# When the left half's last sums, a pair's weight parts, the last x roundings and the first x loads run: four places in the order of a two-layer transformer trunk

## The chip, the cores and the metric

The kernel runs on one core of one Trainium2 chip. The metric is device time in microseconds (us) of one execution. Five engines work side by side, each through its own instructions in order: PE (matrix products), DVE and ACT (elementwise work), POOL (small elementwise work and some transfers) and SP (which only asks for transfers). An engine that waits holds back everything that stands behind the waiting instruction in its own order. Transfers asked for by SP, ACT or POOL run on the core's DMA engines.

## The reference

Two layers over 256 rows of 2048 numbers, everything in float32. Cut to what matters:

```
for l in range(2):
    h = rmsnorm(x, attn_norm_g[l])
    q, k, v, gate_b, gate_c, conv_in = split(h @ w_in[l])       # 6 x 1024 columns
    attn = diff_attention(norm(q), norm(k), v, lam, rel_bias)    # 8 heads
    conv = gate_b * causal_conv3(gate_c * conv_in)
    x = x + concat([attn, conv]) @ w_out[l]
    hm = rmsnorm(x, mlp_norm_g[l]) @ w_up[l]                     # 2048 -> 8192
    x = x + square(relu(hm)) @ w_down[l]                         # 8192 -> 2048
```

## The kernel before

Precision is kept by splitting each float32 operand into a rounded part ("hi") and the remainder ("lo"), so that each product is three matrix products: hi by hi, hi by lo, lo by hi (`TERMS`). ACT writes the hi part (`whi`, `uhi`, `t24h`), then DVE subtracts it from the raw tile for the lo part (`wlo`, `ulo`, `t24l`): lines 311 and 312 for plain weight tiles, 799 and 800 for `w_up`, 823 and 824 for the parts of a seven-product pair, 276 and 278 for the activations `nT` (a transposed, gained and rounded chunk of x).

**Weight tiles.** `Weights.take` hands PE the next hi and lo tile and prepares three further ones (`AHEAD`); the tiles `whi` and `wlo` have three buffers each. The order in which tiles are prepared can differ from that in which they are used: `weights.order`.

**The MLP.** The hidden width is cut into 32 pairs of 128 rows (`NP`). In a first pass the up projection of pair i and the down products of pair i-2 for the left 1024 output columns run together. In a second pass the down products for the right 1024 columns follow from hidden tiles that were stored to memory and are read again (`g`, `f`, `h`). In the second pass 13 pairs (`SEVEN`: 4, 6, 8, 10 ...) are computed as seven half-size products instead of eight: their weights come in three parts, `plain` (b1, b2), `sums` (t1, t3) and `more` (t2, t4), made from the raw tile with DVE lines 837, 840, 841 and rounded on 823 and 824. The other 19 pairs (`PLAIN`) use two plain weight tiles each, 12 matrix products a tile. So before the first seven-product pair PE uses the plain tiles of pairs 0 to 3; they are called tile 1 to tile 8 below. The table `slots` says after which plain tile a part of a seven-product pair is prepared; for the first of these pairs the list in front of it is written out by hand (`[mine[0], mine[1], mine[5], mine[3]]`, for plain, sums, the hidden tile, more).

**The left half's end.** Between the passes, the left columns of x get two additions: `onto` (line 1061, scaled products read from PSUM, the matrix products' accumulators) and then four additions of e tiles (line 1092: 128x512 each). In the last layer the left half is then stored to `out` on SP's queue (line 1096).

**The last chunk of x in the MLP's norm.** `Norm.chunk` transposes a chunk of x on PE and rounds it in four slices k = 0 to 3 with `split_gained` (ACT line 276, DVE line 278). For the last chunk (n = 3), PE's up projection comes to these slices right away, in the order of k.

**The mixer.** q, k and v are projected by halves. `qk_norm` transposes the normed q after a count of ticks (`yield 11`); PE calls `work.tick()` after each six matrix products, and the attention of the first half runs in between on the same ticks. Transposes and scores share three PSUM tiles called `bank`, in rotation: a new one waits until the tile three before it has been read. `Norm.factors` sends the row scales through PE (`rbc`, line 535) after `yield 5`.

**The start.** The first chunk of x is loaded in two halves, then `w_in`'s first tiles slice by slice (line 347, called K tiles here), then the rest (`first_loads`).

PE's order is the program's own; the orders of the other engines come from a scheduler that places instructions by its own model of time, except where the program pins one instruction behind another (`behind`, `late`).

Of the kernel before, what the change touches and what calls it, by code (L numbers as in the profile page):

```python
# [17 lines left out]
D = 2048  # L18
S = 256
# [9 lines left out]
CH = 512  # L29
WC = 256  # L30
KG = 4
# [77 lines left out]
def trunk(ctx: ExitStack, tc: tile.TileContext, x, w_in, w_out, conv_w, q_norm_g, k_norm_g,  # L109
          lambda_q1, lambda_k1, lambda_q2, lambda_k2, subln_g, attn_norm_g, mlp_norm_g,  # L110
          w_up, w_down, rel_bias, selector, out):
    nc = tc.nc
# [40 lines left out]
    ngv = const.tile([NG, P], F32, tag="ngv", name="ngv")  # L153
    load_x(0, 0, CH // 2)
    nc.scalar.dma_start(ngv, attn_norm_g.rearrange("l (k p) -> (l k) p", p=P))
    load_x(0, CH // 2, CH, nc.scalar)

    ones = const.tile([P, P], F32, tag="ones", name="ones")
    nc.vector.memset(ones, 1.0)
# [137 lines left out]
    class Weights:  # L297
# [36 lines left out]
        def plain(self, w, row, c, nk):  # L334

            cols = 2 * CH // nk

            def make():
                raw = self.early.pop(0) if self.early else load()
                return self.halves(raw)  # L340

            def load():
                raw = self.pool.tile([P, nk, cols], F32, tag="raw", name="raw", bufs=RAW)
                src = w[row:row + nk * P, c:c + cols].rearrange("(k p) c -> p k c", p=P)
                if row < KG * P and self.turns and not self.used:
                    for k in range(nk):
                        nc.sync.dma_start(raw[:, k], src[:, k])
                else:
                    self.loads.append(nc.sync.dma_start(raw, src))
                return raw  # L350

            make.load = load
            self.jobs.append(make)
# [89 lines left out]
    class Norm:  # L443
# [9 lines left out]
        def chunk(self, n, wait, banks=None):  # L453
            yield wait
            a = self.tiles[n].open()
            for j in range(2):
                tp = banks[j] if banks else bank(f"tpn{n}_{j}")
                for i in range(2):
                    k = 2 * j + i
                    for t in range(NT):  # L460
                        nc.tensor.transpose(
                            tp[:, i * S + t * P:i * S + (t + 1) * P],
                            xs[n][:, t, k * P:(k + 1) * P], ident)
                with tc.high_priority() if self.which and n == D // CH - 1 else ExitStack():
                    for i in range(2):
                        k = 2 * j + i
                        self.mark = split_gained(
                            a, k, tp[:, i * S:(i + 1) * S], norm_gain(self.which, self.l, n * KG + k))
                self.tiles[n].ready = 2 * j + 2
            self.squares(n)  # L470

# [35 lines left out]
        def factors(self):  # L507
            while self.squared < D // CH or not all(t.ready == KG for t in self.tiles):
                yield 1
            tot = small.tile([P, NT], F32, tag="tot", name="tot")  # L510
            nc.vector.tensor_reduce(tot, self.ss, axis=AX.X, op=ALU.add)
            r = rstd_of(tot, D, "row", NT)
            self.r = small.tile([P, NT], F32, tag="rowf", name="rowf", bufs=2)
            nc.vector.tensor_copy(self.r, r)
            diag = small.tile([P, NT * P + 32], F32, tag="diag", name="diag", bufs=1)
            diag = diag[:, :NT * P].rearrange("p (t c) -> p t c", t=NT)
            if self.which:

                self.scale = small.tile([P, 1], F32, tag="rowf2", name="rowf2")
                nc.vector.tensor_mul(self.scale, r[:, 1:2], r[:, 1:2])  # L520
                ratio = small.tile([P, 1], F32, tag="ratio", name="ratio")
                nc.vector.reciprocal(ratio, r[:, 1:2])
                nc.vector.tensor_mul(ratio, ratio, r[:, 0:1])
                nc.vector.tensor_scalar_mul(diag[:, 0], ident, ratio)
                yield 9
                tp = bank("rbc")
                nc.tensor.matmul(tp[:, :P], ones, diag[:, 0], start=True, stop=True)
                self.ratio = small.tile([P, P], F32, tag="rowb", name="ratiob", bufs=1)
                nc.vector.tensor_copy(self.ratio, tp[:, :P])
                return  # L530
            for t in range(NT):
                nc.vector.tensor_scalar_mul(diag[:, t], ident, self.r[:, t:t + 1])
            yield 5
            tp = bank("rbc")
            nc.tensor.matmul(tp[:, :S], ones, diag.rearrange("p t c -> p (t c)"),
                             start=True, stop=True)
            self.across = small.tile([P, 2, S], F32, tag="rowb", name="rowb", bufs=1)
            nc.vector.tensor_copy(self.across[:, 0], tp[:, :S])
            nc.gpsimd.tensor_tensor(self.across[:, 1], self.across[:, 0], self.across[:, 0],
                                    op=ALU.mult)  # L540
# [2 lines left out]

            return self.across[:, power - 1].unsqueeze(1).to_broadcast([P, 2, S])

    def qk_norm(acc, r, dst, gain, name):

        out_ = []
        for t in range(NT):
            rt = r[:, t:t + 1]  # L550
            sq = wide(f"{name}sq{t}")
            nc.scalar.activation(sq, acc[:, t], AF.Square, scale=rt)
            ms = small.tile([P, NH], F32, tag="ms", name=f"{name}ms{t}")
            nc.vector.tensor_reduce(ms, sq.rearrange("p (g d) -> p g d", d=DK),
                                    axis=AX.X, op=ALU.add)
            f = rstd_of(ms, DK, f"{name}{t}", NH)
            f2 = small.tile([P, NH], F32, tag="f2", name=f"{name}f{t}")
            nc.vector.tensor_scalar_mul(f2, f, rt)
            qn = wide(f"{name}n{t}")
            nc.vector.tensor_tensor(  # L560
                qn.rearrange("p (g d) -> p g d", d=DK),
                acc[:, t].rearrange("p (g d) -> p g d", d=DK),
                f2.unsqueeze(2).to_broadcast([P, NH, DK]), op=ALU.mult)
            out_.append(qn)
        yield 11
        for t in range(NT):
            tp = bank(f"{name}tp{t}")
            for i in range(4):
                nc.tensor.transpose(tp[:, i * P:(i + 1) * P], out_[t][:, i * P:(i + 1) * P], ident)
            tp3 = tp.rearrange("p (h c) -> p h c", c=P)  # L570
            hi, lo = (dst[:, i, :, t * P:(t + 1) * P] for i in range(2))
            nc.scalar.activation(hi, tp3, AF.Copy, scale=gain)
            nc.vector.scalar_tensor_tensor(lo, tp3, gain, hi.bitcast(F32),
                                           op0=ALU.mult, op1=ALU.subtract)
            yield 1
# [113 lines left out]
    def mixer(l, norm, loads):  # L689

        with ExitStack() as scope:
# [24 lines left out]
            for half in range(2):  # L716
# [2 lines left out]
                r = norm.r  # L719
                qT = (spare if half else cats).tile([P, 2, 4, S], F32R, tag=("c1", "s2")[half],  # L720
                                                    name=f"qT{l}{half}")
                work.start(qk_norm(acc, r, qT, q_gain[:, l:l + 1], f"q{l}{half}"))
                acc = linear(f"k{l}{half}", hT, weights)
                kT = (spare if half else cats).tile([P, 2, 4, S], F32R, tag=("c2", "s3")[half],
                                                    name=f"kT{l}{half}")
# [36 lines left out]
    def mlp(l, mnorm, ahead, last):  # L762
# [3 lines left out]
        with ExitStack() as scope:  # L766
# [117 lines left out]
            for i in range(NP - LAG, NP):  # L884
# [7 lines left out]
                   if i not in WHOLE}  # L892
            both = {i: dram.tile([P, 2, 7, P], F32R, name=f"both{l}_{i}") for i in WHOLE}
            plain = [dram.tile([P, 2, 2, 4, P], F32R, name=f"plain{l}_{b}")
                     for b in range((len(PLAIN) + 1) // 2)]
            again = {}

            def load_again(i):
                if i in WHOLE:
                    f = again[i] = fpool.tile([P, 2, 8, P], F32R, tag="f", name="f")  # L900
                    nc.gpsimd.dma_start(f[:, :, 1:], both[i])
                    return
                again[i] = tile_of("h", [P, 8, P], F32, (fpool, "h"), (second, "h"))
                nc.sync.dma_start(again[i][:, 1:].rearrange("p a c -> p (a c)"), hid[i])
# [22 lines left out]
            slots = {}  # L927
            for i in SEVEN:
                before = [j for j in mine if j < where[i]][-4:] if i != SEVEN[0] else [
                    mine[0], mine[1], mine[5], mine[3]]  # L930
                js = [where[i] + k for k in (1, 2, 0, 3)]
                if len(before) == 4 and SEVEN.index(i) and where[SEVEN[SEVEN.index(i) - 1]] > before[0]:
                    before = [before[2], before[2], before[3], before[3]]
                for j, b in zip(js, before):
                    slots.setdefault(b, []).append(j)
# [117 lines left out]
            def block(b):  # L1053
                blocks[b] = apool.tile([P, 2, 2, 4, P], F32R, tag="a", name="g")
                for s in range(min(2, len(PLAIN) - 2 * b)):
                    nc.gpsimd.dma_start(blocks[b][:, s], plain[b][:, s])

            block(0)

# [28 lines left out]
                    work.tick()  # L1088
            for dst, (_, _, p) in zip(left, OWN):
                onto(dst, prods[p], dst)  # L1090
            for dst, v in sums:
                nc.vector.tensor_add(dst, dst, v)

            def store(n):
                for t in range(NT):
                    nc.sync.dma_start(
                        out[0, t * P:(t + 1) * P, n * CH:(n + 1) * CH], xs[n][:, t])

            if last:
                store(0)  # L1100
                store(1)

            w2 = mm.tile([P, 2, CH], F32, tag="mm2", name=f"rt{l}2")
            prods[2], prods[3] = w2[:, 0], w2[:, 1]
# [2 lines left out]
            for i in range(NP):  # L1107
                if i in SEVEN:
# [19 lines left out]
                    if end:  # L1128
                        for dst, v in shared(*right):
                            nc.vector.tensor_add(dst, dst, v)  # L1130
                        if not last:
                            spare = (prods[7], prods[5])
                            work.start(norm.chunk(0, 2, spare), 2)
                            work.start(norm.chunk(1, 2, spare), 6)
                    continue
                b, slot = divmod(PLAIN.index(i), 2)
                if slot == 0 and b == 0:
                    with tc.issue_after(stored[-1].ins):
# [76 lines left out]
```

## Time and profile before

| | |
|---|---|
| median of 3 runs | 2144.89 us (2144.7 to 2146.6) |
| the profiled execution, its own time | 2145.36 us |
| its span, first to last instruction | 2143.5 us |
| mean granted PE clock | 0.999 |
| DVE busy | 1690.7 us (79%) |
| ACT busy | 1292.7 us (60%) |
| DMA, mean over the span | 228 GB/s |

A row of the timeline reads: start in us, duration in us, engine, line, operation, out<-in, count, and in square brackets the idle time before it and what ended it. A row of the chain of waits reads: start, duration, engine, tile and line. "PEld" is PE's weight load, which overlaps its products; "SPq" is a transfer asked for by SP. A row of the waits reads: who waited, for whom, us in total, times, the longest.

### The profile page before, as it was taken

The page shows a single profiled execution, that of the slowest core. Times are in us where ns is not written, and L with a number is a line of the kernel's source. Part 1 is how long each engine was busy: PE and PEld are TensorE (multiplying, and loading weights), DVE is VectorE, ACT ScalarE, POOL GpSimd, SP SyncE. Part 2 cuts the span into 40 slices and gives each one's busy share as a digit, 9 for nine tenths or more (in the row PEclk, how much of TensorE's full clock was granted, in tenths as well). Part 3 has the DMA queues.
Part 4 walks back from the last instruction along what each step waited for, and adds up shares of the span by engine and source line. Part 5 has one row for each costly group of instructions (what it writes and reads, how often), then busy time and mean ns, then how long its engine had stood idle before and what let it go on. Part 6 is the DMA issues. An engine that isn't in the chain of part 4 may idle for free.

```text
span 2143.5 us, 28946 instructions
## 1 busy us (share of the span) xinstructions
PE 2129.0 (99%) x10956; PEld 1811.2 (84%) x10956; DVE 1690.7 (79%) x2307; ACT 1292.7 (60%) x1761; POOL 174.8 (8%) x263
## 2 busy tenths in 40 slices
PE   9999999999999999999999999999999999999999
PEld 7888888888888888878888888888888888888787
DVE  6667656788888888798866776567888888887887
ACT  6556445566666666555565654456666666665553
POOL 1021200000000000100001221000000000001000
PEclk9999999999999999999999999999999999999999
DMA  7655568577777777898466556776777777778992
GB/s 257 187 158 167 182 204 265 184 237 235 238 233 234 239 243 233 262 377 309 151 207 180 157 163 190 221 235 213 226 240 238 225 243 233 240 239 290 362 313 94
DMA packets 291702, 487.79 MB, mean 228 GB/s; under 512 B 10690, under 2 KB 191593, under 8 KB 291561
## 3 DMA queue, kind: packets, MB, share of 16 engines
q1 hardware_dynamic: 266664, 413.14, 61.3%
q0 software_dynamic: 24576, 72.51, 10.2%
q8 instruction: 86, 1.41, 0.3%
q14 instruction: 56, 0.45, 0.1%
q10 hardware_dynamic: 320, 0.28, 0.0%
HBM read 446.42 MB, written 39.48 MB: 227 GB/s over the span
## 4 chain that ended last, share of the span: by engine, by line
PE 95%; DVE 3%; ACT 1%; DMA 1%; issue 1%; POOL 0%; ACTq 0%; DVEq 0%
PE upc L955 31%; PE pr L1005 13%; PE o L396 8%; PE rt L1164 7%; PE rt L1005 6%; PE ci L418 4%; PE gc L418 4%; PE gb L418 4%; PE v L396 4%; PE q L396 4%; PE k L396 3%; DVE wlo L312 1%; PE upw L955 1%; PE up L955 1%; PE pr L1084 1%
## 5 line engine op out<-in xcount | busy, mean ns | idle before, releaser
L311 ACT ACTIVATE whi<-raw 128x1024 fp32r<-128x1024 f32 x324 | 343.0, 1060 | 426.6 <-PE rt L1164 113.4
L312 DVE TENSOR_TENSOR wlo<-raw,whi 128x1024 fp32r<-128x1024 f32 x324 | 398.1, 1231 | 245.3 <-ACT whi L311 240.0
L955 PE MATMUL upc<-nT,uhi 128*128 128x512 f32 x1920 | 477.6, 391 | 0.0
L799 ACT ACTIVATE uhi<-uraw 128x1024 fp32r<-128x1024 f32 x256 | 270.6, 1057 | 267.5 <-PE upc L955 239.9
L800 DVE TENSOR_TENSOR ulo<-uraw,uhi 128x1024 fp32r<-128x1024 f32 x256 | 313.3, 1224 | 127.2 <-ACT uhi L799 115.9
L955 PEld LDWEIGHTS upc<-nT,uhi 128*128 128x128 f32 x1920 | 352.9, 188 | 68.0
L955 PEld LDWEIGHTS upc<-nT,ulo 128*128 128x128 f32 x1920 | 262.0, 191 | 18.6
L955 PE MATMUL upc<-nT,ulo 128*128 128x256 f32 x1920 | 267.8, 283 | 0.0
L1164 PE MATMUL rt<-whi,g 128*128 128x512 f32 x576 | 183.2, 391 | 0.0
L396 PE MATMUL o<-whi,cat 128*128 128x512 f32 x512 | 159.6, 390 | 0.0
L1164 PEld LDWEIGHTS rt<-whi,g 128*128 128x128 f32 x576 | 108.9, 189 | 22.9 <-ACT whi L311 0.3
L1164 PE MATMUL rt<-wlo,g 128*128 128x512 f32 x288 | 113.1, 393 | 4.4 <-DVE wlo L312 4.4
L396 PEld LDWEIGHTS o<-whi,cat 128*128 128x128 f32 x512 | 96.2, 188 | 19.7
L824 DVE TENSOR_TENSOR t24l<-t,t24h 128x1024 fp32r<-128x1024 f32 x86 | 104.9, 1220 | 3.4 <-ACT t24h L823 3.4
L824 DVE TENSOR_TENSOR t13l<-t,t13h 128x1024 fp32r<-128x1024 f32 x86 | 105.2, 1223 | 2.5
L824 DVE TENSOR_TENSOR b2l<-draw,b2h 128x1024 fp32r<-128x1024 f32 x86 | 104.9, 1220 | 0.8 <-ACT b2h L823 0.8
L837 DVE TENSOR_TENSOR t<-draw 128x1024 f32<-128x1024 f32 x86 | 104.9, 1220 | 0.4
L396 PE MATMUL o<-wlo,cat 128*128 128x512 f32 x256 | 99.7, 390 | 0.0
L823 ACT ACTIVATE t24h<-t 128x1024 fp32r<-128x1024 f32 x86 | 90.4, 1051 | 10.2 <-DVE t L841 10.2
L823 ACT ACTIVATE t13h<-t 128x1024 fp32r<-128x1024 f32 x86 | 91.4, 1063 | 4.6 <-PE rt L1005 2.1
L1005 PE MATMUL pr<-t13h,f 128*128 128x512 f32 x240 | 93.9, 391 | 0.0
L823 ACT ACTIVATE b2h<-draw 128x1024 fp32r<-128x1024 f32 x86 | 90.4, 1051 | 3.0 <-PE rt L1005 2.2
(359 smaller groups left out, 3858.2 us busy)
## 6 DMA issues: line engine op xcount, KB each, us to landing
uraw<-in_w_up_dram SPq DMA_DIRECT2D x128, 1024.0 KB, 5.8
raw<-in_w_in_dram SPq DMA_DIRECT2D x190, 512.0 KB, 4.0
draw<-in_w_down_dram SPq DMA_DIRECT2D x90, 1024.0 KB, 6.9
raw<-in_w_down_dram SPq DMA_DIRECT2D x38, 1024.0 KB, 7.3
raw<-in_w_out_dram SPq DMA_DIRECT2D x64, 512.0 KB, 5.4
plain<-f POOLq DMA_DIRECT2D x38, 512.0 KB, 3.7
g<-plain POOLq DMA_DIRECT2D x38, 512.0 KB, 8.8
both<-f POOLq DMA_DIRECT2D x12, 896.0 KB, 4.4
```

Of the source, the lines that this page charges most:

```text
L311: self.splits.append((nc.scalar.activation(hi, raw, AF.Copy), nc.vector.tensor_sub(lo, raw, hi.bitcast(F32))))
L312: nc.vector.tensor_sub(lo, raw, hi.bitcast(F32))))
L396: nc.tensor.matmul(acc[:, t], a.ap[:, pa, k % KG, t * P:(t + 1) * P], (hi, lo)[pw][:, j], start=(k == 0 and n == 0), stop=(k == nk - 1 and ...
L418: nc.tensor.matmul(acc[:, f, 0] if part else acc[:, f], wt[:, k % 4, fs], a.ap[:, 0, k % KG] if part else a.ap[:, :, k % KG], start=(part ...
L799: nc.scalar.activation(hi, src, AF.Copy)
L800: nc.vector.tensor_sub(lo, src, hi.bitcast(F32))
L823: keep(nc.scalar.activation(hi, src, AF.Copy))
L824: keep(nc.vector.tensor_sub(lo, src, hi.bitcast(F32)))
L837: keep(nc.vector.tensor_sub(t[:, 0:2], raw[:, :, 1], raw[:, 0]))
L955: nc.tensor.matmul(acc[:, 0] if part else acc, wt[:, k], a.ap[:, 0, k % KG] if part else a.ap[:, :, k % KG], start=(part == 0 and kh == 0 ...
L1005: nc.tensor.matmul(prods[n], f[:, pa, a], b[pw], start=(start and m == 0), stop=(stop and m == 2))
L1164: nc.tensor.matmul(prods[p], blocks[b][:, slot, pa, 2 * k + t], w[pw][:, n], start=(i == PLAIN[0] and k == 0 and m == 0), stop=False)
```

## The change

Five edits; no arithmetic changes.

1. The left half's four last additions are taken out of the place between the passes. `finish_left` does one of them when PE comes to each of the plain pairs 7, 9, 11 and 13 of the second pass, pinned behind the newest lo tile of the plain weights on DVE, and in the last layer then stores what is complete.
2. The first seven-product pair's parts are prepared later: `sums` after tile 3 instead of tile 2, `more` after tile 7 instead of tile 4.
3. In the last chunk of the MLP's norm, the rounding of slice k is pinned behind that of slice k-1.
4. `rbc` goes to PE 9 ticks after its input was asked for instead of 5, and in the second half of the heads the transposes of q come 13 ticks after the projection instead of 11.
5. The second half of x's first chunk is asked for by SP behind the first K tile, and no more by ACT.

The pin on `load_again` (POOL) leaves POOL's order as it was.

```diff
-    load_x(0, CH // 2, CH, nc.scalar)
...
                         nc.sync.dma_start(raw[:, k], src[:, k])
+                        if row == k == 0:
+                            load_x(0, CH // 2)
...
-                        self.mark = split_gained(
-                            a, k, tp[:, i * S:(i + 1) * S], norm_gain(self.which, self.l, n * KG + k))
+                        pinned = self.which and n == D // CH - 1 and k
+                        with behind(*(self.mark if pinned else ())):
+                            self.mark = split_gained(
+                                a, k, tp[:, i * S:(i + 1) * S],
+                                norm_gain(self.which, self.l, n * KG + k))
...
-            yield 5
+            yield 9
...
-        yield 11
+        yield wait
...
-                work.start(qk_norm(acc, r, qT, q_gain[:, l:l + 1], f"q{l}{half}"))
+                work.start(qk_norm(acc, r, qT, q_gain[:, l:l + 1], f"q{l}{half}",
+                                   11 + 2 * half))
...
-                    nc.gpsimd.dma_start(f[:, :, 1:], both[i])
+                    with behind(*g_loads[-1:]):
+                        nc.gpsimd.dma_start(f[:, :, 1:], both[i])
...
-                    mine[0], mine[1], mine[5], mine[3]]
+                    mine[0], mine[2], mine[5], mine[6]]
...
-            for dst, v in sums:
-                nc.vector.tensor_add(dst, dst, v)
...
-            if last:
-                store(0)
-                store(1)
+            def finish_left():
+                dst, v = sums.pop(0)
+                with behind(weights.splits[-1][1]):
+                    nc.vector.tensor_add(dst, dst, v)
+                if last and len(sums) < 2:
+                    store(1 - len(sums))
...
+                if i > SEVEN[1] and sums:
+                    finish_left()
```

DVE at the start of the first layer's second pass, from the last `onto` on, before (`x_83` and `x_84` are the two left chunks of x, `t` the sums of the first seven-product pair):

```order
L1061 SCALAR_TENSOR_TENSOR x_84<-pr_8439,rowf_3839,x_84 128x512
L1092 TENSOR_TENSOR x_83<-x_83,e_8432 128x512
L312 TENSOR_TENSOR wlo<-raw,whi 128x1024
L1092 TENSOR_TENSOR x_83<-x_83,e_8430 128x512
L1092 TENSOR_TENSOR x_84<-x_84,e_8433 128x512
L312 TENSOR_TENSOR wlo<-raw,whi 128x1024
L1092 TENSOR_TENSOR x_84<-x_84,e_8432 128x512
L837 TENSOR_TENSOR t<-draw 128x1024
L312 TENSOR_TENSOR wlo<-raw,whi 128x1024 x2
L824 TENSOR_TENSOR t13l<-t,t13h 128x1024
L840 TENSOR_TENSOR t<-t,draw 128x512
L841 TENSOR_TENSOR t<-draw,t 128x512
```

And now, from the same `onto` on (line numbers of the changed kernel: 1067 was 1061, 311 was 312, 842, 845 and 846 were 837, 840 and 841, 829 was 824):

```order
L1067 SCALAR_TENSOR_TENSOR x_84<-pr_8439,rowf_3839,x_84 128x512
L311 TENSOR_TENSOR wlo<-raw,whi 128x1024
L842 TENSOR_TENSOR t<-draw 128x1024
L311 TENSOR_TENSOR wlo<-raw,whi 128x1024 x2
L829 TENSOR_TENSOR t13l<-t,t13h 128x1024
L845 TENSOR_TENSOR t<-t,draw 128x512
L311 TENSOR_TENSOR wlo<-raw,whi 128x1024
L846 TENSOR_TENSOR t<-draw,t 128x512
L311 TENSOR_TENSOR wlo<-raw,whi 128x1024
L829 TENSOR_TENSOR t24l<-t,t24h 128x1024
```

The four additions are gone from this stretch, and the lo part of tile 7, the second single `wlo` after `t13l`, stands ahead of `t24l` where it stood behind it.

ACT in the same stretch before, where the first `x5` are the hi parts of tiles 2 to 6 and the `x3` those of tiles 7 to 9:

```order
L996 ACTIVATE f<-h 128x896
L311 ACTIVATE whi<-raw 128x1024 x5
L823 ACTIVATE t13h<-t 128x1024
L823 ACTIVATE t24h<-t 128x1024
L311 ACTIVATE whi<-raw 128x1024 x3
L823 ACTIVATE t24h<-t 128x1024
```

And now:

```order
L1002 ACTIVATE f<-h 128x896
L310 ACTIVATE whi<-raw 128x1024 x4
L828 ACTIVATE t13h<-t 128x1024
L310 ACTIVATE whi<-raw 128x1024 x2
L828 ACTIVATE t24h<-t 128x1024
L310 ACTIVATE whi<-raw 128x1024 x3
```

The hi part of tile 7 stood behind `t24h` and now stands ahead of it.

ACT where the last chunk of x is rounded in the first layer, before (`tpn_0_3808` holds slices 0 and 1, `tpn_1_3817` slices 2 and 3; `uhi` is a weight tile of the up projection):

```order
L799 ACTIVATE uhi<-uraw 128x1024
L276 ACTIVATE nT_3_3807<-tpn_0_3808,gains 128x256
L276 ACTIVATE nT_3_3807<-tpn_1_3817,gains 128x256
L799 ACTIVATE uhi<-uraw 128x1024
L276 ACTIVATE nT_3_3807<-tpn_0_3808,gains 128x256
L276 ACTIVATE nT_3_3807<-tpn_1_3817,gains 128x256
```

And now (275 was 276, 804 was 799):

```order
L804 ACTIVATE uhi<-uraw 128x1024
L275 ACTIVATE nT_3_3807<-tpn_0_3808,gains 128x256
L804 ACTIVATE uhi<-uraw 128x1024
L275 ACTIVATE nT_3_3807<-tpn_0_3808,gains 128x256
L275 ACTIVATE nT_3_3807<-tpn_1_3817,gains 128x256 x2
```

The slices went 0, 2, weight tile, 1, 3 and now go 0, weight tile, 1, 2, 3; on DVE likewise slice 0 alone stands ahead of that tile's lo part, and slices 1, 2 and 3 behind it.

More of the change, by code (lines that the diff above doesn't have):

```diff
@@ L544, in bc, with qk_norm @@
             return self.across[:, power - 1].unsqueeze(1).to_broadcast([P, 2, S])
-    def qk_norm(acc, r, dst, gain, name):
+    def qk_norm(acc, r, dst, gain, name, wait=11):
         out_ = []
@@ L895, in mlp @@
                      for b in range((len(PLAIN) + 1) // 2)]
-            again = {}
+            again, g_loads = {}, []
             def load_again(i):
@@ L1055, in block @@
                 for s in range(min(2, len(PLAIN) - 2 * b)):
-                    nc.gpsimd.dma_start(blocks[b][:, s], plain[b][:, s])
+                    g_loads.append(nc.gpsimd.dma_start(blocks[b][:, s], plain[b][:, s]))
             block(0)
```

## The prediction

> **What bounds the kernel now.** I read the page first, its busy times: PE works through nearly the whole span.
>
> ```profile
> PE 2129.0 (99%) x10956; PEld 1811.2 (84%) x10956; DVE 1690.7 (79%) x2307; ACT 1292.7 (60%) x1761; POOL 174.8 (8%) x263
> ```
>
> No edit takes a product from PE, so only PE's idle time is to be had: 2143.5 - 2129.0 = 14.5 us. Second I read what PE waited for.
>
> ```profile
> PE rt L1164 <- DVE wlo L312: 4.4, 2, 2.2
> PE up L955 <- DVE nT L278: 1.5, 2, 0.7
> PE tpb L494 <- DMA x<-in_x_dram: 1.2, 1, 1.2
> ...
> PE q11tp L569 <- DVE cat L656: 0.5, 1, 0.5
> PE q01tp L569 <- DVE cat L656: 0.5, 1, 0.5
> PE rbc L535 <- DVE diag L532: 0.4, 1, 0.4
> ```
>
> These six rows are the places of the five edits, and they sum to 8.5 us: the waits alone cannot give more than 0.4%. Each place is judged by what ends last there, by its chain and its timeline.
>
> **The second pass: 6.5 us.** The chain of waits from 895 to 960 us, first layer:
>
> ```profile
> 907.73 2.06 DVE x L1061 x3
> 909.79 0.46 DVE x L1092
> ...
> 911.52 1.21 DVE x L1092 x2
> ...
> 913.86 0.60 DVE x L1092
> ...
> 920.37 1.07 ACT t24h L823
> ...
> 923.87 1.23 DVE wlo L312
> 925.14 5.52 PE rt L1164 x23
> ...
> 935.42 5.44 PE rt L1164 x24
> ```
>
> For 17 us DVE sets the pace, and the four additions (L1092) hold 0.46 + 1.21 + 0.60 = 2.3 us of that chain. ACT then rounds t24h ahead of tile 7's hi part, and PE waits 2.2 us for tile 7's lo part. An undisturbed stretch runs 24 products in 5.44 us, 0.227 each; the 23 after the wait took 5.52 instead of 5.21. Place one costs 2.2 + 0.3 = **2.5 us**.
>
> In the second layer the same wait costs more, by its chain row and the granted clock:
>
> ```profile
> 1988.49 6.97 PE rt L1164 x23
> ```
> ```profile
> 925.00:930.00 5.00, 4.86 (x21) 4.04 (x22) 3.87 (x6) 2.18 (x3) 0.00 (x0) 1.00 1.07 407
> 1988.00:1992.00 4.00, 3.51 (x9) 2.79 (x10) 2.87 (x4) 0.00 (x0) 0.00 (x0) 0.57 1.07 407
> ```
>
> The column after POOL is the granted clock: 1.00 behind the first wait, 0.57 behind the second. 2.2 + (6.97 - 5.21) = **4.0 us**, of which some 1.5 are the clock.
>
> Without the additions, from PE's first product of the pass, two loads that SP asked for, and ACT's hi part of tile 9:
>
> ```profile
> 906.20 0.39 PE L1164 MATMUL rt<-whi,g 128*128 128x512 f32 x1
> 907.84 0.37 SPq L809 DMA_DIRECT2D raw<-in_w_down_dram  x1
> 913.89 0.37 SPq L809 DMA_DIRECT2D raw<-in_w_down_dram  x1
> ```
> ```profile
> 924.72 1.06 ACT L311 ACTIVATE whi<-raw 128x1024 fp32r<-128x1024 f32 x1 [1.39 <-DMA raw<-in_w_down_dram]
> ```
>
> With the additions gone, DVE goes from 909.8 through the lo parts of tiles 3 to 6 (about 1.2 us each), t (1.2), t13l (1.2) and the two half-size t (1.3): 8.5 us, to 918.3. Tile 7's hi part can start when PE is done with tile 4, whose buffer it takes: 906.2 + 4 x 2.72 = 917.1 (12 products a tile). Its lo part is done by 919.6; PE wants it at 906.2 + 6 x 2.72 + 0.23 = 922.7. Tile 8, behind t24h and t24l, comes at about 922.5 to 923.5 and is wanted at 925.5. What could still be late is memory. The load asked for at 913.89 was waited for until 924.7, 10.8 us. At that pace the one of 907.84, for tiles 7 and 8, lands at 918.7 and the lo part is done at 921.0: still 1.7 us early. Both waits go, and 2.5 + 4.0 = 6.5 us with them. The additions come back one by one, 0.65 us each, in stretches where DVE is that far ahead: tile 9, whose hi part is the row above, is used only at 935.4. The t parts moved later have the same cover: `more` is ready by about 925 and wanted at about 931 (eight tiles and 14 products from 906.2). The pins add no wait of their own. The stores leave the place where SP held them among the weight loads; four of 256 KB at the 407 GB/s above are 0.65 us each, less than that lead.
>
> On the clock, the Trainium skill ("TensorE: Matmul & The Clock Gate", section "HAM oscillation — how this bites in real kernels") says that only idle gaps above some 3.4 us take the clock down. The trace differs: a gap of 2.2 us did in one layer, and not in the other. By the rule, the 1.5 us of lost clock would not belong to this wait and could stay, and the sum would be 1.5 less.
>
> **The last roundings of x: -0.4 us, a loss.** The timeline at the first layer's place:
>
> ```profile
> 398.59 1.06 ACT L799 ACTIVATE uhi<-uraw 128x1024 fp32r<-128x1024 f32 x1 [1.59 <-PE up L955]
> 399.28 1.33 PE L955 MATMUL up<-nT,uhi 128*128 128x512 f32 x5
> 399.55 0.82 ACT L276 ACTIVATE nT<-tpn,gains 128x256 fp32r<-128x256 f32 x2
> 399.68 1.23 DVE L800 TENSOR_TENSOR ulo<-uraw,uhi 128x1024 fp32r<-128x1024 f32 x1 [0.34 <-ACT uhi L799]
> 400.82 0.87 DVE L278 SCALAR_TENSOR_TENSOR nT<-tpn,gains,nT 128x256 fp32r<-128x256 f32 x2
> 401.35 0.98 PE L955 MATMUL up<-nT,uhi 128*128 128x512 f32 x3 [0.75 <-DVE nT L278]
> ```
>
> PE's fifth product here takes slice 0, then it waits for slice 1. Slice 1 stands on ACT behind a weight tile (uhi) that waits for PE itself until 398.59, and on DVE behind that tile's ulo, until 400.82. The order after the change leaves slice 1 behind both. What it moves is slice 2, which was done early and now stands behind slice 1. So PE starts again at 401.35 as before, slice 2 comes at 401.7 and slice 3 at 402.1 (0.4 a slice by the row of two in 0.87), where PE would have taken its last product at about 401.9. I take 0.2 us a layer lost, 0.4 in all; from above, the whole wait with its restart, 0.95 a layer, could go: +1.9.
>
> **The transposes of q: 1.1 us.**
>
> ```profile
> 126.49 0.66 PE L569 MATMUL q01tp<-ident,q01n 128*128 128x128 f32 x4 [0.54 <-DVE cat L656]
> ```
> ```profile
> 119.75 0.74 DVE L615 SCALAR_TENSOR_TENSOR s<-s,c 128x128 f32<-128x128 f32 x2
> 126.89 0.42 DVE L597 CUSTOM_DVE_ANT_0 s<-sc,bias 128x256 f32<-128x256 f32 x1
> ```
>
> The transpose takes the `bank` that DVE frees with `cat`, just before 126.49. Two ticks later, six products and the transposes of the probabilities (ptp) stand ahead of it. ptp's input is L615's, done at 120.5, and it now takes that bank, after six products of 0.227 from 125.95 (126.49 - 0.54), at 127.3: free by then. q's transposes come at 129 and take the first scores' bank, read by 127.3 (the L597 row). 0.54 us a layer goes. The q parts come some 2 us later and are used a whole projection later.
>
> **rbc: 0.** Its 0.4 us goes in the first layer, but PE then comes the sooner to this:
>
> ```profile
> 42.91 1.06 ACT L311 ACTIVATE whi<-raw 128x1024 fp32r<-128x1024 f32 x1 [4.04 <-DMA raw<-in_w_in_dram]
> ```
> ```profile
> 45.28 0.19 PEld L396 LDWEIGHTS k<-wlo,nT 128*128 128x128 f32 x1 [0.50 <-DVE wlo L312]
> ```
>
> ACT waits 4 us for a weight load and PE for the result; rbc 24 products (5.4 us) later still runs ahead of 45.28. The end there is the load's, so I count nothing, at most 0.4. The second layer's rbc waited for nothing.
>
> **The start: 0.9 us.**
>
> ```profile
> 4.99 1.12 PE L494 MATMUL tpb<-ident,x 128*128 128x128 f32 x4 [1.19 <-DMA x<-in_x_dram]
> ```
> ```profile
> DMA packets 691, 0.78 MB, mean 224 GB/s; under 512 B 55, under 2 KB 547, under 8 KB 691
> ...
> q10 hardware_dynamic: 261, 0.23, 20.9%
> ```
> ```profile
> 10.00:15.00 5.00, 4.81 (x24) 3.59 (x23) 2.88 (x6) 3.19 (x7) 0.00 (x0) 1.00 1.05 393
> ```
>
> From 1.5 to 5.0 us, 0.78 MB moved, 0.23 of them on ACT's queue (q10): nearly all of that is x's second half, beside the first half for which PE waited. Behind the first K tile those 0.2 MB no longer come in between; at 224 GB/s that is 0.9 us. The bounds are 1.19, PE's whole wait, and 0, if the landing is latency; the 0.4 us that SP needs to ask is hidden as long as DMA is full (share 1.05 up to 15 us). PE is busy 4.81 of 5 us there: it sets the pace, so I let the gain pass.
>
> The Trainium skill ("DMA: Bandwidth & Descriptors", section "Issuing engines are not separate DMA queues") says that transfers of several engines interleave on the same DMA engines, and that asking from several saves only the time to ask. By it alone this edit would give no bandwidth and cost SP's 0.4 us; the rows agree with the interleaving, which is what the 0.9 rests on.
>
> **The sum.** 6.5 - 0.4 + 1.1 + 0 + 0.9 = 8.1 us from the profiled execution's own 2145.36: 2137.3. That execution stands 0.5 above the median of the runs (2144.89); against the median, **2136.8**.
>
> **Rivals.**
> - The roundings work as meant and both waits at `up` go: 0.4 + 1.9 = 2.3 more, 2134.5. Against it: the order on ACT and DVE above. 0.11.
> - The lost clock belongs to no wait and stays: 2138.3. For it: one layer of two kept its clock. 0.06.
> - The start's gain ends at the load at 42.91, if that keeps its hour: 2137.7. 0.10.
> - Half of the second pass's waits stays, because memory lands later still than 10.8 us after its asking (by 1.7 us for tile 7) and t24h then pushes tile 8: 2140.0. For it: DMA is full there (share 1.07). 0.10.
> - The parts do not do what they say: DVE is as late as before, since each saved addition lets a load be asked for sooner and the full DMA gives it back. PE's waits shift to later tiles: within a microsecond or two of 2144. 0.09.
> - Slower: an addition pinned behind the newest lo tile is late on DVE, SP holds the last layer's store for it, and the weight load behind the store comes late. It decides from the lead, about 10 us between tile 9's rounding and its use: below it, nothing. At 3 us of lateness beyond the lead on each of four stores, 12 us eat the 8.1 and 4 more: 2149. Against it: each store's addition stands on DVE ahead of the next b parts, whose draw buffer SP waits for anyway. 0.06.
>
> **How the numbers follow.** The forecast has 0.48, rivals 0.52. From 2144.89, 0.2% is 4.3 us, about what a measurement of this kernel can tell from no change: faster means below 2140.6. Forecast, first three rivals and half of the fourth: 0.80 faster; the other half and the fifth: 0.14 the same; 0.06 slower. Downwards the bounds are the roundings (2.3), rbc (0.4) and the start (0.3): 2133.8. Upwards they are the start (0.9) and the clock (1.5), 2139.2, and half the second pass's waits, 2140.0; with a little of the fifth rival, 2141. The range is 2133.8 to 2141.0.
>
> **What would show it.** Right: no wait of `rt` on wlo at the start of either second pass, granted clock 1.00 behind it, no wait of q01tp and q11tp, `tpb` starting at about 4.1, and `up` still waiting for nT some 0.75 us, or in two pieces. Wrong: `up` without a wait; a wait of `rt` on whi or wlo at tile 8 or at the first seven-product pair; k's wait at 45 us that has not moved with the start; SP rows in the last pass whose weight loads come later behind a store.

## The result and the profile after

The changed kernel takes 2139.64 us (median of 10 runs, 2138.86 to 2139.98) against 2144.82 (10 runs, 2144.36 to 2146.76): the ratio is 0.9973 with an interval of 0.9963 to 0.9983, 0.27% less. The forecast was 2136.8, the range 2133.8 to 2141.0. The profiled execution went from 2145.36 to 2139.43, its span from 2143.5 to 2137.7 us.

The page of the changed kernel, busy times, and then all that PE waited for:

```profile
PE 2127.5 (100%) x10956; PEld 1809.3 (85%) x10956; DVE 1689.8 (79%) x2307; ACT 1292.7 (60%) x1761; POOL 174.8 (8%) x263
```
```profile
PE up L961 <- DVE nT L277: 2.5, 4, 0.7
PE q L397 <- DVE wlo L331: 1.5, 2, 1.3
PE warm L166 <- DVE ones L158: 1.0, 1, 1.0
PE k L397 <- DVE wlo L311: 0.4, 1, 0.4
PE rt L1158 <- DVE x L1067: 0.4, 1, 0.4
PE tpb L498 <- DMA x<-in_x_dram: 0.2, 1, 0.2
```

Of the six places, `rt` on wlo and both transposes of q are gone, as forecast. The wait of rbc is gone too, but a wait of k of 0.36 us that this list did not have before has come. `up` now waits four times instead of twice, and q has a wait of 1.3 us that was not there. The same instruction of PE in both traces shows where its lead was won and lost (us, minus is earlier):

| stretch | gain or loss |
|---|---|
| first transposes of x (`tpb`) | -1.05 |
| `tpb` at 24.9 us, after the new wait of q | back to +0.05 |
| k's wait at 45 us | on to -0.31 |
| q01tp, q11tp | -0.48, -0.47 |
| last roundings of x, layers 1 and 2 | +0.94, +0.93 |
| second pass, layer 1 and layer 2 | -2.54, -3.87 |

The -0.31 and the rows behind it sum to -5.8, the whole change of the span.

**Second pass.** Windows of the changed kernel at the two places (the column after POOL is the granted clock), and the timeline at tile 7:

```profile
920.00:925.00 5.00, 5.00 (x24) 4.14 (x23) 4.25 (x4) 2.81 (x4) 0.00 (x0) 1.00 1.08 405
1984.00:1988.00 4.00, 4.00 (x19) 3.17 (x18) 3.76 (x5) 2.09 (x3) 0.00 (x0) 1.00 1.09 408
1988.00:1992.00 4.00, 4.00 (x19) 3.32 (x18) 3.96 (x5) 2.13 (x3) 1.06 (x2) 1.00 1.07 403
```
```profile
919.65 1.06 ACT L310 ACTIVATE whi<-raw 128x1024 fp32r<-128x1024 f32 x1 [3.82 <-DMA raw<-in_w_down_dram]
920.75 1.23 DVE L311 TENSOR_TENSOR wlo<-raw,whi 128x1024 fp32r<-128x1024 f32 x1 [2.79 <-ACT whi L310]
922.90 0.39 PE L1173 MATMUL rt<-wlo,g 128*128 128x512 f32 x1
```

PE works through both stretches at clock 1.00. Tile 7's lo part is done at 921.98 and used at 922.90, so the lead is 0.9 us and not the 1.7 of the forecast: the load asked for at 907.99 was waited for until 919.65, 11.7 us instead of 10.8. Behind tile 7 the additions come back, and in the second layer the stores go out with them. PE's lead stays at 2.39 us from there to the end of the first layer's second pass, and in the second layer at 5.77 to 5.82 up to the last product. So the late additions, their pins and the stores cost nothing here, and the rival that made the kernel slower did not come.

**Last roundings.** The timeline of the changed kernel, first layer:

```profile
400.03 0.87 DVE L277 SCALAR_TENSOR_TENSOR nT<-tpn,gains,nT 128x256 fp32r<-128x256 f32 x2
400.56 0.89 PE L961 MATMUL up<-nT,uhi 128*128 128x512 f32 x2 [0.75 <-DVE nT L277]
400.93 0.47 ACT L275 ACTIVATE nT<-tpn,gains 128x256 fp32r<-128x256 f32 x1 [1.35 <-DVE nT L277]
401.44 0.48 DVE L277 SCALAR_TENSOR_TENSOR nT<-tpn,gains,nT 128x256 fp32r<-128x256 f32 x1 [0.54 <-ACT nT L275]
401.98 0.50 PE L961 MATMUL up<-nT,uhi 128*128 128x512 f32 x1 [0.52 <-DVE nT L277]
```

The old wait of 0.75 is there, and a second of 0.52 for slice 3: its part on ACT starts only when DVE is done with slice 2 (row of 400.93), which lies in the same accumulator bank.

**The start.** Before:

```profile
20.45 0.41 DVE L242 TENSOR_TENSOR lprod<-lamv 1x256 f32<-1x256 f32 x1 [1.79 <-DMA lamv<-in_lambda_k_dram]
```

And after:

```profile
3.94 1.11 PE L498 MATMUL tpb<-ident,x 128*128 128x128 f32 x4 [0.16 <-DMA x<-in_x_dram]
20.50 0.41 DVE L241 TENSOR_TENSOR lprod<-lamv 1x256 f32<-1x256 f32 x1 [3.08 <-DMA lamv<-in_lambda_k_dram]
22.29 0.50 PE L397 MATMUL q<-wlo,nT 128*128 128x512 f32 x1 [1.33 <-DVE wlo L331]
```

DVE takes its instructions in order, and `lprod`, a product of the small lambda vectors, stands among the K tiles' lo parts. Its loads land when they did, so DVE waits 1.29 us longer, and PE waits 1.33 us for the lo part behind it (p7_lambda_later tests this).

### The profile page after: what moved, and what is told of

Its sections match the earlier page's. It is cut to its first block, busy times and chain, and to the rows that moved or that the text cites. A ratio compares the mean times of both kernels' runs of the same rounds, so it can differ in the third digit from the quotient of the medians.

```text
span 2137.7 us, 28947 instructions
## 1 busy us (share of the span) xinstructions
PE 2127.5 (100%) x10956; PEld 1809.3 (85%) x10956; DVE 1689.8 (79%) x2307; ACT 1292.7 (60%) x1761; POOL 174.8 (8%) x263
## 3 DMA queue, kind: packets, MB, share of 16 engines
q8 instruction: 86, 1.41, 0.3%
## 4 chain that ended last, share of the span: by engine, by line
PE 97%; DVE 1%; DMA 1%; ACT 0%; issue 0%; SPq 0%; ACTq 0%
PE upc L961 31%; PE pr L1011 14%; PE rt L1173 9%; PE o L397 8%; PE rt L1011 6%; PE ci L419 4%; PE gc L419 4%; PE gb L419 4%; PE v L397 4%; PE k L397 4%; PE q L397 4%; PE upw L961 1%; PE pr L1090 1%; PE up L961 1%; PE sc L595 1%; PE av L634 0%
## 5 line engine op out<-in xcount | busy, mean ns | idle before, releaser
L1173 PEld LDWEIGHTS rt<-whi,g 128*128 128x128 f32 x576 | 108.2, 188 | 22.3
```

The lines of the kernel that those rows point to most:

```text
L1173: nc.tensor.matmul(prods[p], blocks[b][:, slot, pa, 2 * k + t], w[pw][:, n], start=(i == PLAIN[0] and k == 0 and m == 0), stop=False)
```

## The experiments

Each was run beside the kernel before, whose medians were 2145.35 (20 runs, first four), 2145.04 (10, next four) and 2145.04 (13, last four). The intervals are wide because the kernel before has two levels (last section), so kernels are compared by medians of one group and by their traces.

**The second pass: both edits, and each alone.** On the kernel before, edits 1 and 2:

```diff
-            for dst, v in sums:
-                nc.vector.tensor_add(dst, dst, v)
...
+            def finish_left():
...
-                    mine[0], mine[1], mine[5], mine[3]]
+                    mine[0], mine[2], mine[5], mine[6]]
```

> The kernel before with the late sums and the new slots of the first pair's parts, nothing else. Theory: these two edits carry the second pass alone, 2.5 us in layer 1 and 3.9 in layer 2, so about 6.4 us below the kernel before (2138.4); no wait of rt on wlo at the start of either second pass, and granted clock 1.00 there in both layers. Rival (the lost clock of layer 2 belongs to no wait): only some 5 us below, and a clock below 1.00 somewhere in layer 2.

2138.55 us (6 runs), ratio 0.9971 [0.9959, 0.9982]. Against the kernel before's executions at clock 0.999 (median 2144.79) that is 6.2 us, and the clock was 1.000 in all six. The expected absence of a wait did not hold in the profiled execution, the slowest of the six (2140.38). Its timeline at tile 7 of the first layer:

```profile
921.59 1.06 ACT L311 ACTIVATE whi<-raw 128x1024 fp32r<-128x1024 f32 x1 [6.39 <-DMA raw<-in_w_down_dram]
...
922.71 0.50 PE L1168 MATMUL rt<-whi,g 128*128 128x512 f32 x1 [0.51 <-ACT whi L311]
923.96 0.50 PE L1168 MATMUL rt<-wlo,g 128*128 128x512 f32 x1 [0.76 <-DVE wlo L312]
```

This is another cause than before: tile 7's load, asked for at 907.35, was waited for until 921.59, 14.2 us. It cost this execution some 1.9 us against the changed kernel's gain in the same place.

The late sums alone (only `finish_left` and what goes with it):

```diff
-            for dst, v in sums:
-                nc.vector.tensor_add(dst, dst, v)
...
+            def finish_left():
```

> The kernel before with the late sums alone; the parts of the first pair keep their old slots. Theory (tile 7 is late because 2.3 us of additions and 1.1 us of t24h stand ahead of it together, and a margin of some 2 us is needed): either edit alone takes the wait away, so about 6.4 us below the kernel before, as with both. Rival (each edit is worth its own durations): the additions take 2.3 us off a layer's chain and t24h's 1.1 stays, so a wait of rt of 0.5 to 1 us stays in each layer.

2139.09 us (7 runs), 0.9970 [0.9959, 0.9981], 5.7 us below 2144.79, with no wait of 2 us in the profile and none at tile 7. PE's weight load waits at an earlier tile, for tile 3's lo part, and 0.35 us goes there in each layer:

```profile
911.75 0.19 PEld L1167 LDWEIGHTS rt<-wlo,g 128*128 128x128 f32 x1 [0.50 <-DVE wlo L312]
```

The new slots alone, with the pin on `load_again` as in p1_sums_and_slots (the late sums alone go without it):

```diff
-                    mine[0], mine[1], mine[5], mine[3]]
+                    mine[0], mine[2], mine[5], mine[6]]
```

> The kernel before with the new slots alone (t24h behind two more weight tiles on ACT); the four additions stay in place at once. Theory (either edit alone suffices): tile 7's hi part starts at about 917 and its lo part is done at about 921.6 where PE wants it at 922.7, so the wait of rt goes and the time is about 6.4 us below the kernel before. Rival (the additions are the cause): about 1 us a layer off, a wait of rt of about 1.1 us stays in each layer, and the time is 2 to 3.5 us below the kernel before.

2139.42 us (7 runs), 0.9972 [0.9961, 0.9983], 5.4 us below. The timeline has a small wait at an earlier tile in each layer:

```profile
914.62 0.50 PE L1165 MATMUL rt<-wlo,g 128*128 128x512 f32 x1 [0.30 <-DVE wlo L312]
...
1976.02 0.50 PE L1165 MATMUL rt<-wlo,g 128*128 128x512 f32 x1 [0.30 <-DVE wlo L312]
```

With its restart it takes 0.57 us a layer. So either edit alone takes the 2.2 us waits and the lost clock away; together they bring 0.5 to 0.9 more by the medians, and the earlier waits are where the traces place it. The rivals, which gave each edit its own durations, fall.

**The ticks alone,** on the kernel before:

```diff
-            yield 5
+            yield 9
...
-        yield 11
+        yield wait
```

> The kernel before with rbc four ticks and q's second transposes two ticks later, nothing else. Theory: the waits of q01tp and q11tp (0.54 and 0.5) go and 0.3 of rbc's 0.38 is kept at k's wait of 45 us: 1.2 to 1.3 us below the kernel before. Rival (rbc's wait is given back whole at k's wait, as the prediction had it): 0.95 to 1.1 us, k's wait at 45 us longer by 0.4.

2143.82 us (11 runs), 0.9995 [0.9986, 1.0003]: the ratio does not tell it from none. At equal clock it does: at 0.999 the medians are 2143.62 (5 runs) and 2144.79 (11), at 0.998 2145.35 (5) and 2146.54 (9), 1.2 us each. ACT's wait for k's weights and the wait of PE's weight load for k, from its timeline:

```profile
42.21 1.06 ACT L311 ACTIVATE whi<-raw 128x1024 fp32r<-128x1024 f32 x1 [3.73 <-DMA raw<-in_w_in_dram]
...
44.58 0.19 PEld L396 LDWEIGHTS k<-wlo,nT 128*128 128x128 f32 x1 [0.84 <-DVE wlo L312]
```

The same weight load waited 0.50 us before, so k's wait grew by 0.34, as the rival said. Rbc's own wait, 0.38, is thereby given back nearly whole. The 1.2 us at equal clock is the theory's size, but it is only 0.1 above the rival's, and ACT's load also comes sooner where rbc stands as before. In the late sums alone, with rbc's old wait of 0.38 still there:

```profile
42.16 1.06 ACT L311 ACTIVATE whi<-raw 128x1024 fp32r<-128x1024 f32 x1 [3.23 <-DMA raw<-in_w_in_dram]
```

So what q's transposes brought is shown (0.50 and 0.47 us in the trace); that moving rbc brought anything is not.

**The start's old order,** put back into the changed kernel:

```diff
+    load_x(0, CH // 2, CH, nc.scalar)
...
-                        if row == k == 0:
-                            load_x(0, CH // 2)
```

> The changed kernel with the old order of x's first loads. Theory (the start's 1.05 us at the first transposes is given back at 22.3, where DVE's lprod holds the K tiles until the lambda loads have landed at 20.5, and the first transposes' hour scatters by up to a microsecond from execution to execution anyhow): the same as the changed kernel within 0.4 us, tpb of chunk 2's second half at 24.5 to 24.9. Rival (the prediction's 0.9 us): 0.9 us slower than the changed kernel.

2139.4 us (7 runs), 0.9971 [0.9959, 0.9982], against 2139.64 and 2139.54 for the changed kernel: the edit brings nothing in this place.

**The roundings' pins taken out** of the changed kernel:

```diff
-                        pinned = self.which and n == D // CH - 1 and k
+                        pinned = False
```

> The changed kernel without the pins between the last roundings of x. Theory (the pins cost 0.95 us a layer, since slice 3 on ACT waits for DVE on slice 2, which shares its bank): 1.9 us faster than the changed kernel, about 2137.7, up waiting once a layer, 0.75 us, as in the kernel before. Rival (the prediction's size): 0.4 us faster.

2137.21 us (5 runs), 0.9961 [0.9948, 0.9974]: 2.2 below p5_old_start of the same group, nearer to 1.9 than to 0.4. The trace gives 0.95 and 0.94 in the two layers, and `up` waits once a layer again.

**lprod and lps later,** in the changed kernel:

```diff
-        nc.vector.tensor_copy(gains, vps[:, :ROWS])
+        gained = nc.vector.tensor_copy(gains, vps[:, :ROWS])
...
+        yield 8
...
-        nc.vector.tensor_mul(prod, lamv[:, 0:2], lamv[:, 2:4])
+        with behind(gained):
+            nc.vector.tensor_mul(prod, lamv[:, 0:2], lamv[:, 2:4])
```

> The changed kernel with lprod pinned behind the copy of the gains on DVE (33 us instead of 20.5) and the product with the lambdas (lps) eight ticks later on PE. Theory (lprod, waiting for its loads, is what ends the start's gain): the wait of q at 22.3 goes, tpb at 24.9 comes at 23.6 to 23.9, and the time is 0.7 to 1.3 us less than the changed kernel's. Rival (the load behind ACT's wait of 42.6 keeps its hour): the wait at 22.3 goes, k's wait at 45 us grows by as much, and the time stays within 0.3.

2138.0 us (5 runs), 0.9964 [0.9951, 0.9977], 1.4 below p5_old_start. From its timeline:

```profile
23.35 0.60 PE L499 MATMUL tpb<-ident,x 128*128 128x128 f32 x4
...
31.78 0.40 DVE L242 TENSOR_TENSOR lprod<-lamv 1x256 f32<-1x256 f32 x1
```

`lprod` waits for nothing, the wait of q at 22.3 is gone, that `tpb` comes 1.58 us sooner, and 1.41 of it is still there at 51 us. The theory's place is shown; the gain is a little more than its 0.7 to 1.3.

**The weight tile behind the roundings,** in the changed kernel, with the pins between the slices out:

```diff
-                    nc.scalar.activation(hi, src, AF.Copy)
-                    nc.vector.tensor_sub(lo, src, hi.bitcast(F32))
+                    with behind(*(mnorm.mark if (i, c, kh) == (1, 0, 0) else ())):
+                        nc.scalar.activation(hi, src, AF.Copy)
+                        nc.vector.tensor_sub(lo, src, hi.bitcast(F32))
```

> The changed kernel without the pins between the slices, and in place of them the fifth weight tile of the up projection (its uhi and ulo) pinned behind the last rounding. Theory (slices 1 and 3 are late because that uhi, which waits for PE until 397.8, and its ulo stand ahead of them): both waits of up go in both layers, 2.5 to 3.4 us less than the changed kernel, 2136.2 to 2137.1; the weight tile is wanted at 406 only. Rival (the weight tile becomes late in its turn): a wait of upw or up for uhi or ulo near 403 to 406 and a gain below 2 us.

2135.57 us (5 runs), 0.9953 [0.9939, 0.9967], 3.8 below p5_old_start. Its timeline at the place:

```profile
397.97 0.92 ACT L275 ACTIVATE nT<-tpn,gains 128x256 fp32r<-128x256 f32 x2 [1.55 <-DVE nT L277]
398.80 1.05 ACT L805 ACTIVATE uhi<-uraw 128x1024 fp32r<-128x1024 f32 x1
...
399.07 0.48 DVE L277 SCALAR_TENSOR_TENSOR nT<-tpn,gains,nT 128x256 fp32r<-128x256 f32 x1
...
398.71 2.00 PE L962 MATMUL up<-nT,uhi 128*128 128x512 f32 x8
```

PE runs all eight products without a wait; the last slice is done at 399.55, and the weight tile moved behind it is ready long before PE comes to it. The trace gives 1.98 and 1.99 us in the layers. The gain is above the theory's 2.5 to 3.4: a wait also draws out the products beside it. In the changed kernel the same eight took 1.33 + 0.89 + 0.50 = 2.72 us beside 1.27 of idle time. In this execution 0.8 goes back at tile 7 of the first layer's second pass, where `rt` waits 0.49 for wlo, so its own time, 2136.37, lies above the median.

**The changed kernel again,** unedited, for the last three:

> The changed kernel itself, beside the next three on one chip. Theory and rival alike: 2139.6 within 0.4; a control for the differences below.

2139.54 us (8 runs), 0.9975 [0.9964, 0.9985]. Its profiled execution (2140.22) has a wait that the first one did not have. Timeline at tile 7:

```profile
921.23 1.06 ACT L310 ACTIVATE whi<-raw 128x1024 fp32r<-128x1024 f32 x1 [5.43 <-DMA raw<-in_w_down_dram]
...
922.32 1.23 DVE L311 TENSOR_TENSOR wlo<-raw,whi 128x1024 fp32r<-128x1024 f32 x1 [4.40 <-ACT whi L310]
...
923.60 0.50 PE L1173 MATMUL rt<-wlo,g 128*128 128x512 f32 x1 [0.58 <-DVE wlo L311]
```

The load asked for at 907.96 was waited for until 921.23, 13.3 us, and the lead of 0.9 was gone. It cost this execution 0.9 us by the landmark behind it. The same place in all ten profiled executions that have edits 1 and 2, first layer, against the first profile of the changed kernel:

| run | from asking for tile 7's load to ACT's hi part, us | lost at tile 7, us |
|---|---|---|
| the changed kernel, p6, p7, p5 | 11.7, 11.9, 12.3, 12.3 | 0 |
| p12, p11, p10 | 12.7, 12.9, 12.9 | 0.3, 0.5, 0.5 |
| p8, p9 | 13.2, 13.3 | 0.8, 0.9 |
| p1 | 14.2 | 1.9 |

In the second layer it is 11.5 to 12.6 us, and at most 0.1 is lost. So after the change the first layer's tile 7 waits for memory in six executions of ten.

**lprod later, with x's old order of loads** (the edits of p7_lambda_later and p5_old_start together):

```diff
+    load_x(0, CH // 2, CH, nc.scalar)
...
+        with behind(gained):
```

> The changed kernel with lprod and lps later, and with the old order of x's first loads. Theory A (the start's order gives nothing even where lprod no longer stands behind it, since the first transposes scatter between 3.9 and 5.0 us with either order): the same as with lprod later alone, 1.2 to 1.7 us below the changed kernel. Rival (the prediction's 0.9 us was right and only hidden by lprod): 0.3 to 0.8 us below the changed kernel.

2138.92 us (6 runs), 0.9971 [0.9959, 0.9982]: 0.6 below p9_changed_again, which is the rival's band. But three of its six runs lie at 2138.2 to 2138.5 and three at 2139.4 to 2140.0, and the profiled one, with its `tpb` at 23.21, is as early as with the new order (23.35). Whether the new order makes an early start likelier stays open.

**Pins kept, weight tile behind them** (the edit of p8_weights_behind without taking the pins out):

```diff
+                    with behind(*(mnorm.mark if (i, c, kh) == (1, 0, 0) else ())):
```

> The changed kernel with its pins kept, and with the fifth weight tile of the up projection pinned behind the last rounding as well. Theory (the pins cost because slices 1 and 3 stood behind the weight tile, not by their order): no wait of up, or one below 0.2 us a layer, 3.5 to 4.1 us below the changed kernel. Rival (the order of the slices itself is slow, since slices 1 and 3 wait on ACT for DVE on slices 0 and 2): a wait of up of some 0.5 us a layer stays, 2.5 to 3 us below the changed kernel.

2136.66 us (5 runs, 2135.32 to 2137.27), 0.9959 [0.9947, 0.9972], 2.9 below p9_changed_again. By PE's waits the theory holds: none of `up`, though PE's weight load for slice 3 still waits 0.37 in the first layer. By the median the rival's band does. The trace gives 1.75 us in each layer, 0.23 less than without the pins (the eight products of 398.71 take 2.22 us instead of 2.00), and about 0.5 goes back at tile 7 of the second pass. So the pins cost little once the weight tile is out of their way.

**Both gains together** (edits of p7_lambda_later and p8_weights_behind):

```diff
+        with behind(gained):
...
+                    with behind(*(mnorm.mark if (i, c, kh) == (1, 0, 0) else ())):
```

> The changed kernel with both gains put together: no pins between the slices, the fifth weight tile behind the last rounding, lprod and lps later. Theory (the two places are independent): 4.1 and 1.6 us below the changed kernel, 2133.9. Rival (PE, coming sooner, waits for memory at tile 7 of the second passes or at k's weights of 45 us): 2135 to 2136, with a wait of rt for wlo in one of the layers or of k at 45 us.

2135.33 us (5 runs, 2134.41 to 2135.94), 0.9954 [0.9941, 0.9966]: 4.2 below the changed kernel and the fastest of all, but short of 2133.9 and in the rival's band. The rival's mechanism is there in small: PE's weight load waits at tile 7 of the first layer, and 0.28 us goes back there; k's wait is not in the profile.

```profile
920.67 0.19 PEld L1175 LDWEIGHTS rt<-wlo,g 128*128 128x128 f32 x1 [0.41 <-DVE wlo L312]
```

Most of what it lacks is at the start. Its timeline there:

```profile
5.07 1.48 PE L166 MATMUL warm<-ones 128*128 128x128 f32 x6
6.36 0.80 PE L398 MATMUL q<-whi,nT 128*128 128x512 f32 x1
...
24.61 0.60 PE L499 MATMUL tpb<-ident,x 128*128 128x128 f32 x4
```

And that of p7_lambda_later:

```profile
5.01 0.83 PE L166 MATMUL warm<-ones 128*128 128x128 f32 x6
6.26 0.49 PE L398 MATMUL q<-whi,nT 128*128 128x512 f32 x1 [0.41 <-ACT whi L331]
```

The same six products took 1.48 and 0.83 us, and `tpb` came 1.26 us later than in the other (24.61 against 23.35); 1.05 of it is left behind k's wait. At the roundings it has its 1.98 us in both layers. So the places are independent, and most of the missing 1.4 lies, by the traces, in PE's pace at the start (last section).

## Why the forecast was right in direction and 2.8 us too low

- **Second pass, 6.5 us: right.** The traces give 6.4, the executions at equal clock 6.2 for the two edits alone. Wrong in it was the lead: "still 1.7 us early" was 0.9, since memory took 11.7 us for tile 7 and not 10.8, and 12.7 to 14.2 in six of ten profiled executions. What the fourth rival asked for does happen there, mostly at 0.3 to 0.9 us and once at 1.9, in one layer and not as half of the old waits in both. It is luck that the first profile of the changed kernel shows none of it. And the two edits are not two halves of the gain: either removes the wait.
- **The clock, 1.5 us: right.** The lost clock belongs to the wait. The Trainium skill ("TensorE: Matmul & The Clock Gate", section "HAM oscillation — how this bites in real kernels") asks for gaps above some 3.4 us; the runs do not agree, as the last section shows with their numbers.
- **Last roundings, -0.4: the mechanism was right, the size was not; -1.9.** The step that failed is "slice 3 at 402.1 (0.4 a slice by the row of two in 0.87)". That row is of two slices in different banks. Slices 2 and 3 share one, so slice 3 takes ACT's 0.47 and DVE's 0.48 one after the other, and PE stops a second time: 0.95 a layer instead of 0.2. p6_roundings_unpinned shows it (2.2 us back). That slice 1 stays behind the weight tile was right, and p8_weights_behind shows that this was the cause of the old wait too.
- **q's transposes, 1.1: right,** 0.95 by the traces.
- **rbc, 0: not refuted.** 0.3 us was won in this place, but not shown to be by the edit. ACT's load was there at 42.61 instead of 42.91. In p1, p2 and p3, which keep rbc's place and its wait of 0.38, it was there at 42.43, 42.16 and 42.41, and PE won 0.17, 0.38 and 0.30 there. With the edit the weight load of k waits 0.78 instead of 0.50, or 0.84 with the ticks alone. "The end there is the load's" fits all of this; the load's hour is what scatters.
- **The start, 0.9: 0.** Two steps failed. "it sets the pace, so I let the gain pass" overlooked `lprod`, whose wait on DVE stood at 20.45 in the trace of before; p7_lambda_later shows that it ends the gain. And the 1.19 us came from one execution: in the other six with the old order, PE does not wait for x at the first `tpb`, and where it waits (0.3 to 0.7 us in four of them) it is in `gps`, for the norm gains' load. Seven profiled executions with each order of x's loads give this (means of starts in us; the last column only of kernels with `lprod` in its old place, six and five):

| order of x's loads | first `tpb` | second `tpb` | `tpb` of chunk 2's end |
|---|---|---|---|
| old | 4.31 (3.89 to 4.99) | 8.96 (8.08 to 9.75) | 24.69 |
| new | 4.05 (3.85 to 4.17) | 8.68 (8.03 to 9.38) | 24.77 |

The ranges overlap; 0.3 us is won on the mean, and nothing is left of it at 24.7.

The terms with their measured sizes, 6.4 - 1.9 + 0.95 + 0, make 5.5 instead of 8.1. With some 0.3 of the load's scatter at k that is the change of the span, 5.8. The median moved by 5.2, since the profiled executions do not lie at their medians. The forecast's direction rests on the second pass alone, whose mechanism was right; the roundings and the start were mis-sized by 1.5 and 0.9 on the same side.

## What to carry to other kernels

A pin that puts instructions in order must also go past what stands ahead of the first of them: in the kernel before, the weight tile's hi and lo parts, not the slices' order, made PE wait; moving that tile took the wait away where ordering the slices added one. Before a gain is let pass, follow the engines that feed PE down their order to the next instruction that waits for something unmoved, such as `lprod` for its loads. A wait seen in one execution at the start or for a load while the DMA engines are full is a draw from a spread: look at it in several executions before it becomes a term.

## What the runs showed of the hardware

**A wait of 2.2 us costs clock in some executions and not in others.** The kernel before has two levels in its 43 executions beside the experiments: 27 with a mean granted clock of 0.999 (median 2144.79) and 16 with 0.998 (2146.63), 1.84 us apart. With the ticks alone, the same two levels appear, and one execution of 1.000 at 2141.91, 1.7 below the median at 0.999. That fits none, one or both of the two waits losing some 1.7 to 1.8 us; in both profiled executions with these waits, before and p4_ticks_only, the second layer's wait lost it (a granted clock of 0.57 and 0.66 from 1988 to 1992 us) and the first layer's did not. Of 76 executions of kernels without these waits, 74 have 1.000; of the other two, one (p8_weights_behind) lost its clock only behind PE's last product, and the second was not profiled. Why a wait of the same length loses clock in one execution and not in another was not tried.

**PE starts at half pace, and the column of the granted clock does not show it.** In nine of the 14 profiled executions PE's first products of q last 0.8 us, as in p12_best above, until they last 0.39. Where PE idled at most 0.23 us ahead of the first `tpb` (six executions) the full pace was there by 7.3 us, in the other eight (0.26 to 1.19 us) only between 7.6 and 9.5. The idle time was not varied by itself, so this is what went together and not a shown cause. A window of p12_best, with the granted clock at 1.00:

```profile
6.00:7.00 1.00, 1.00 (x4) 0.55 (x3) 0.97 (x3) 0.78 (x2) 0.00 (x0) 1.00 0.93 234
```

The Trainium skill ("TensorE: Matmul & The Clock Gate", section "What's actually happening") says that PE begins at half rate and goes to full rate after some 3.4 us of sustained work, counted in windows that do not start with the kernel. The traces agree with the half rate and with the scatter. It was worth 1.26 us between p7_lambda_later and p12_best. In seven of the eight the idle time is that of `gps`, which waits for the norm gains' load; an earlier load of them was not tried.
